# A one-core encoder trunk: DRAM copies of weight sums moved to ScalarE's queue, a fixed load order, and a fused closing step

## The chip, the cores and the metric

The kernel runs on one core of a Trainium2 chip. TensorE (PE) multiplies matrices into PSUM, VectorE (DVE) and ScalarE (ACT) do element-wise work, GpSimd (POOL) does a little of it and issues the accumulating DMAs, and SyncE (SP) does nothing but issue DMAs. ACT can issue DMAs too. Each engine runs its own instructions in the order that the program's scheduler has given them, and waits at semaphores for the others. The metric is the device time of one launch in microseconds, as the median of several runs.

## The reference: four layers over 256 tokens

The input is 256 tokens of 1024 channels in float32. Four layers follow each other. Each adds a token mixer and then a feed-forward block, both behind an RMS norm; a last RMS norm with a gain closes the trunk. Layers 0 and 3 mix by retention (four heads, per-head norm with `ret_gn_w` and `ret_gn_b`, a silu gate), layer 1 by a Conformer convolution of width 31, layer 2 by stick-breaking attention with 16 heads. The feed-forward block, which the change mostly touches, is

```
h = relu(rms_norm(x, norm_ffn[i]) @ ffn_w1[i])      # 256 x 4096
x = x + (h * h) @ ffn_w2[i]                         # 256 x 1024
```

All weights are float32, 220 MB in all, and every one of them passes from DRAM through the core in one launch.

## The kernel before

**Weights.** The host lays the weights out in the order of use, in 220 chunks of 128x2048 floats (1 MB), each of two units of 128x1024. `unit_hi` (lines 347 to 390) loads a chunk on SP's queue when its first unit is due (line 362) into one of three `raw` buffers, makes the high part of a unit on ACT (`wh`, line 388, rounding to the format that PE multiplies), and `unit_lo` makes the rest on DVE (`wl`, line 395). There are five `wh` and five `wl` buffers. A float32 product is three products of parts: high by high, high by low, low by high. Activations are split the same way.

**Down projection.** `down` (from line 775) computes `(h*h) @ ffn_w2`. Some of its 16 blocks of 256 rows are done plainly (lists `MIXED` and `REST`), the others (`FAST`) by a Strassen scheme: 7 products of 128x128 by 128x512 blocks instead of 8, three matmuls each (line 780). For that a unit needs, beside its blocks b21, b11, b22, b12, the sums t1 = b11+b12, t3 = b12+b22, t2 = t1+b22, t4 = t2+b21. `make_sums` (lines 399 to 411) has the DMA engines form m of the first three in a DRAM tile `sums`, long before they are needed: line 405 copies b12 into one or two places (256 or 512 KB, on SP's queue, kept in program order), line 406 adds b11 and b22 to it by an accumulating DMA on POOL's queue, and for m = 3 lines 408 and 409, also POOL's, make t2. `AHEAD` lists at which chunk's load each such job is issued: one list for each layer, one entry for each `FAST` block. There are 31 jobs: 7 with m = 2 in layer 0, 6 with m = 1 in layer 1, 9 with m = 3 each in layers 2 and 3. When the `FAST` unit itself is loaded, 768 KB come from the weights (line 362), t1 from `sums` (line 365), and t3 and t2 into two of ten buffers called `t` (line 368). t4 is added on DVE (line 459), and lines 431 and 432 split the sums.

**Closing.** After the last `FAST` block the sums that were gathered in PSUM are combined (lines 823 to 830). C[0,1] and C[1,1] are completed there; C[0,0] and C[1,0], the left half of the columns for the two halves of the tokens, still take the plain blocks of `REST`. Then line 857 adds `e1` to C[0,0] and line 858 subtracts `u` from C[1,0] on DVE, in place in PSUM, and `scaled` (line 872) multiplies both by the row scale `r2` on ACT into `t` buffers. PE meanwhile does the first `REST` block of the right half, and then transposes the scaled tiles (line 885), which line 892 adds to the residual. The last layer (`final`) has its own hook, which squares and scales instead of transposing.

**Order of the work.** A scheduler orders the instructions of each engine by a timing model; within stages marked as manual the order is the program's. In stick-breaking attention PE and ACT are manual and DVE is not. `keep_in_program_order` keeps an instruction behind the one that the program traced just before it on the same engine, and says nothing of later ones, which may still be drawn ahead; `issue_after` puts a block's instructions behind a given one of the same engine. In the retention layers line 1147 loads the gain and the bias of a head's norm (`gn`) on SP's queue, in program order.

Of the kernel before, what the change touches and what calls it, by code (L numbers as in the profile page):

```python
# [12 lines left out]
ALU = mybir.AluOpType  # L13
# [48 lines left out]
AHEAD = {  # L62
    0: [(n, 2) for n in (26, 27, 28, 38, 40, 42, 45)],
    1: [(n, 1) for n in (81, 83, 85, 87, 89, 91)],
    2: [(n, 3) for n in (110, 112, 114, 116, 118, 121, 129, 133, 137)],
    3: [(n, 3) for n in (167, 170, 173, 176, 179, 182, 192, 196, 199)],
}
OUT_ORDER = [(kb, p) for g in (0, 2) for kb in range(4) for p in (g, g + 1)]
# [185 lines left out]
class Trunk:  # L254
# [92 lines left out]
    def unit_hi(self, key):  # L347
        nc = self.nc
        assert PLAN[self.un] == key, (PLAN[self.un], key)
        o = self.un % UPC  # L350
        if o == 0:
            n = self.un // UPC
            if n < len(self.first):
                self.rawt = self.first[n]
            else:
                self.rawt = self.raw.tile([P, RAWW], F32, name=self.nm("raw"), tag="raw")
                h = 1024 if n < 4 else UPC * 1024
                made = self.made.get((key[1], key[3])) if key[2] == "f" else None
                if made:
                    h = 1536  # L360
                for a in range(0, UPC * 1024 // h * h, h):
                    nc.sync.dma_start(self.rawt[:, a : a + h], self.w_d[n][:, a : a + h])
                if made:
                    d, m = made
                    nc.sync.dma_start(self.rawt[:, h : h + 512], d[:, :512])
                    self.fetched = [self.tmp() for _ in range(m - 1)]
                    for a, t in enumerate(self.fetched):
                        nc.sync.dma_start(t, d[:, 512 * (a + 1) : 512 * (a + 2)])
            for _ in range(min(2, len(self.later))):
                self.later.pop(0)()  # L370
            if self.un // UPC in JOBS:
                self.make_sums(*JOBS[self.un // UPC])
            if self.un // UPC in DECAY:
                i = DECAY.index(self.un // UPC) % RH
                if i == 0:
                    self.decay = self.cp.tile([P, RH * 384], F32, name=self.nm("decay"), tag="decay")
                n = i * 384
                self.tc.keep_in_program_order(
                    nc.sync.dma_start(self.decay[:, n : n + 384], self.cst_d[:, CCOL["D"] + n : CCOL["D"] + n + 384])
                )  # L380
        o = self.un % UPC
        src = self.rawt[:, o * 1024 : (o + 1) * 1024]
        hi = self.wp.tile([P, 1024], F32R, name=self.nm("wh"), tag="wh")
        lo = self.wp.tile([P, 1024], F32R, name=self.nm("wl"), tag="wl")
        n = 512 if self.un < 2 * UPC else 1024
        cuts = [slice(i, i + n) for i in range(0, 1024, n)]
        for s in cuts:
            nc.scalar.copy(hi[:, s], src[:, s])  # L388
        self.un += 1
        return hi, lo, src, cuts  # L390
# [8 lines left out]
    def make_sums(self, l, kb, m):  # L399
        nc = self.nc  # L400
        w = self.w_d[CHUNK[l, kb]]
        d = self.dram.tile([P, m * 512], F32, name=self.nm("sums"), tag=f"sums{l}_{kb}", bufs=1)
        n = min(m, 2)
        src = w[:, 1536:2048].unsqueeze(1).to_broadcast([P, n, 512])
        self.tc.keep_in_program_order(nc.sync.dma_start(v3(d[:, : n * 512], n, 512), src))
        nc.gpsimd.dma_start(d[:, : n * 512], w[:, 512 : 512 + n * 512], accum_op=ALU.add)  # L406
        if m == 3:
            nc.gpsimd.dma_start(d[:, 1024:], d[:, :512])
            nc.gpsimd.dma_start(d[:, 1024:], w[:, 1024:1536], accum_op=ALU.add)
        self.made[l, kb] = d, m  # L410
# [364 lines left out]
    def down(self, i, h, fast, begin, hook):  # L775
        nc = self.nc

        def triple(o, a, w, start=False, stop=False):
            for n, (l, r) in enumerate(((a[0], w[0]), (a[0], w[1]), (a[1], w[0]))):
                mm = nc.tensor.matmul(o, l, r, start=start and n == 0, stop=stop and n == 2, skip_group_check=True)  # L780
                self.tc.keep_in_program_order(mm)
            self.end = mm.ins

        def block(k, t):
            return tuple(h[k][:, o + t * P : o + (t + 1) * P] for o in (0, S))

        def plain(kb, c):
            w = self.unit(("ffn_w2", i, "a", kb, c * 512))
            return [tuple(v3(x, 2, 512)[:, kk] for x in w) for kk in range(2)]

        C = {}
        quick, mixed, late_kb = FAST[i], MIXED[i], REST[i]
        self.ahead = {}
        for _ in range(2):
            self.sum_ahead(i)
        for kb in mixed:
            if kb not in quick:
                for c in range(2):
                    w = plain(kb, c)
                    if kb == mixed[0]:  # L800
                        for t in range(2):
                            C[t, c] = self.acc()
                            if begin:
                                begin(c, t, C[t, c])
                    for kk in range(2):
                        for t in range(2):
                            triple(C[t, c], block(2 * kb + kk, t), w[kk], kb == mixed[0] and kk == 0 and not begin)
                continue
            w = self.fast_unit("ffn_w2", i, kb)
            s3, s2, s4 = fast[kb]  # L810
            a, z = kb == quick[0], kb == quick[-1]
            if a:
                p1, p5, p7, p6 = own = [self.mis() for _ in range(4)]
            k = 2 * kb
            for o, x, y in (
                (p1, block(k, 0), w[0]), (C[0, 0], block(k + 1, 0), w[1]), (C[0, 1], s4, w[2]), (p5, block(k, 1), w[3]),
                (p7, s3, w[4]), (p6, s2, w[5]), (C[1, 0], block(k + 1, 1), w[6]),
            ):
                extra = o in own
                triple(o, x, y, a and extra, z and extra)  # L820

        e1, e5, v, u, vq, uq = (self.bigt() for _ in range(6))
        nc.scalar.copy(e1, p1)
        nc.scalar.copy(e5, p5)
        nc.vector.tensor_sub(v, p6, e1)
        nc.vector.tensor_sub(u, v, p7)
        nc.vector.tensor_add(vq, v, e5)
        nc.vector.tensor_add(uq, u, e5)
        nc.vector.tensor_add(C[0, 1], C[0, 1], vq)
        closed = nc.vector.tensor_add(C[1, 1], C[1, 1], uq).ins  # L830

        hook(C, "gain")
        if i == 0:
            self.strip_t = []

            def fetch():
                d = self.strips[len(self.strip_t)]
                o = self.bigt()
                self.tc.keep_in_program_order(nc.sync.dma_start(o, d))
                self.strip_t.append(o)  # L840

            self.later = [fetch] * len(self.strips)

        for c in range(2):
            w, late = {}, late_kb[-2] if c else late_kb[-1] + 1
            steps = [(kb, kk, t) for kb in late_kb if kb < late for kk in range(2) for t in range(2)]
            steps += [(kb, kk, t) for t in range(2) for kb in late_kb if kb >= late for kk in range(2)]
            for kb, kk, t in steps:
                if kb not in w:
                    with self.tc.issue_after(closed) if c else nullcontext():  # L850
                        w[kb] = plain(kb, c)
                if c:
                    hook(C, (kb, kk, t))
                triple(C[t, c], block(2 * kb + kk, t), w[kb][kk], stop=(kb, kk) == (late_kb[-1], 1))
            if c == 0:
                with self.tc.issue_after(closed):
                    nc.vector.tensor_add(C[0, 0], C[0, 0], e1)
                    nc.vector.tensor_sub(C[1, 0], C[1, 0], u)
                hook(C, 0)
        return C  # L860


    def middle(self, i, h, fast, sums, nxt):
# [28 lines left out]
            nc.vector.tensor_add(x, x, a)  # L892

        def hook(C, at):
            if at == 0:
                for t in range(2):
                    scaled(C, t, 0)
                self.norm_begin()
            if at == (REST[i][1], 0, 0):
                for t in range(2):  # L900
# [26 lines left out]
    def final(self, i, h, fast):  # L927
# [12 lines left out]
                ))  # L940

        def hook(C, at):
            if at == "gain":
                for c in range(2):
                    gain.append(self.bigt())
                    nc.sync.dma_start(gain[c], self.fin_d[:, c * 512 : (c + 1) * 512])
            if at:
                return
            for t in range(2):
                q, g, sm = self.tmp(), self.tmp(), f[:, t : t + 1]  # L950
                nc.scalar.activation(out=q, in_=C[t, 0], func=AF.Square, accum_out=sm)
# [906 lines left out]
```

## Time and profile before

| | us |
|---|---|
| median of 3 runs | 1330.94 |
| the runs | 1328.36, 1330.94, 1335.21 |
| time of the profiled execution | 1330.45 |
| its span, first to last instruction | 1328.7 |
| PE busy / DVE busy / ACT busy / POOL busy | 1311.1 / 1088.6 / 882.6 / 212.5 |

The profile is of one execution. A row of the timeline gives the start in us from the span's start, the duration in us, the engine, the line of the kernel, the operation, out<-in, the shapes, how many instructions are merged, and in brackets the idle time of the engine before it and what ended it. "SPq" is a DMA issue on SP; its duration is that of the issue, not of the transfer. A row of waits gives who waited for whom, the total in us, how often, and the longest. In the chain of waits a row is start, duration, what. In a list of DMA issues the last number is the median time from issue to landing, in us.

### The profile page before, as it was taken

The numbers are of one execution on the slowest core, as the hardware profiler recorded it, in microseconds if no ns is written. First come the engines' busy times: TensorE is split into PE (matmuls) and PEld (weight loads), VectorE is DVE, ScalarE is ACT, GpSimd is POOL, SyncE is SP. The second block draws the span as 40 slices with busy tenths as digits, with TensorE's granted clock in tenths as the row PEclk, the third lists the DMA queues.
The fourth block names the chain that finished last, engine by engine and source line by source line (L and its number), as shares of the span: only waits on it lengthen the run. The fifth ranks groups of instructions, "written<-read, shape, count | busy, mean of one in ns | idle before, by whom it ended". The sixth has DMA issues, their size and how long they took to land.

```text
span 1328.7 us, 20675 instructions
## 1 busy us (share of the span) xinstructions
PE 1311.1 (99%) x7661; PEld 1127.1 (85%) x7661; DVE 1088.6 (82%) x1903; ACT 882.6 (66%) x1451; POOL 212.5 (16%) x240
## 2 busy tenths in 40 slices
PE   9999999999999999999999999999999999999998
PEld 7988888888889898888778898888888888888876
DVE  7988777888888588789878588888898767899977
ACT  7555546886666477866758678867765554667764
POOL 3554421000009120010011011000121110100000
PEclk9999999999999999999999999999999999999999
DMA  8566786966675658688698658777568987687673
GB/s 310 206 217 231 244 281 194 298 210 227 233 300 145 206 192 242 220 247 260 208 256 214 210 185 281 245 257 268 214 207 247 267 247 237 196 256 249 226 278 111
DMA packets 76038, 309.58 MB, mean 233 GB/s; under 512 B 8480, under 2 KB 13728, under 8 KB 52512
## 3 DMA queue, kind: packets, MB, share of 16 engines
q1 hardware_dynamic: 63552, 274.43, 59.4%
q0 software_dynamic: 11520, 31.20, 12.3%
q10 hardware_dynamic: 864, 2.62, 0.6%
q8 instruction: 60, 0.98, 0.3%
q14 instruction: 42, 0.34, 0.1%
HBM read 301.57 MB, written 45.45 MB: 261 GB/s over the span
## 4 chain that ended last, share of the span: by engine, by line
PE 95%; DMA 2%; DVE 1%; ACT 1%; issue 1%; SPq 0%; ACTq 0%; DVEq 0%
PE acc L643 22%; PE acc L780 17%; PE acc L639 11%; PE mis L780 7%; PE acc L1207 5%; PE acc L1209 5%; PE acc L1208 5%; PE acc L623 3%; PE acc L624 3%; PE acc L625 3%; PE mis L643 2%; DMA raw<-in_w 1%; PE acc L1375 1%; PE mis L639 1%; PE acc L1508 1%; DMA big<-in_gn 1%
## 5 line engine op out<-in xcount | busy, mean ns | idle before, releaser
L395 DVE TENSOR_TENSOR wl<-raw,wh 128x1024 fp32r<-128x1024 f32 (+1 forms) x406 | 495.4, 1232 | 105.0 <-ACT wh L388 103.5
L388 ACT CAST wh<-raw 128x1024 fp32r<-128x1024 f32 (+1 forms) x406 | 418.4, 1041 | 201.0 <-PE acc L1209 61.7
L643 PE MATMUL acc<-z,wh 128*128 128x512 f32 x1152 | 399.4, 393 | 0.0
L639 PE MATMUL acc<-z,wl 128*128 128x256 f32 x1152 | 317.9, 281 | 0.0
L643 PEld LDWEIGHTS acc<-z,wh 128*128 128x128 f32 x1152 | 214.2, 187 | 47.1
L639 PEld LDWEIGHTS acc<-z,wl 128*128 128x128 f32 x1152 | 216.9, 189 | 2.4 <-DVE t L668 0.3
L780 PE MATMUL acc<-wh,big 128*128 128x512 f32 x632 | 208.6, 391 | 0.0
L780 PEld LDWEIGHTS acc<-wh,big 128*128 128x128 f32 x632 | 118.6, 188 | 24.4
L1207 PE MATMUL acc<-wh,z 128*128 128x512 f32 x352 | 139.1, 396 | 0.0
L1209 PE MATMUL acc<-wh,z 128*128 128x512 f32 x352 | 137.8, 391 | 0.0
L1208 PE MATMUL acc<-wl,z 128*128 128x512 f32 x352 | 137.7, 391 | 0.0
L780 PE MATMUL acc<-wl,big 128*128 128x512 f32 x316 | 123.0, 389 | 0.0
L667 ACT COPY t<-acc 128x256 f32<-128x256 f32 x154 | 53.0, 371 | 51.6 <-PE acc L643 50.0
L431 ACT CAST wh<-t 128x512 fp32r<-128x512 f32 x102 | 60.3, 619 | 39.2 <-PE acc L780 12.0
L1207 PEld LDWEIGHTS acc<-wh,z 128*128 128x128 f32 x352 | 66.6, 189 | 15.4 <-issue 2.2
L1209 PEld LDWEIGHTS acc<-wh,z 128*128 128x128 f32 x352 | 66.4, 189 | 14.9 <-issue 0.8
L1208 PEld LDWEIGHTS acc<-wl,z 128*128 128x128 f32 x352 | 66.6, 189 | 13.4
L432 DVE TENSOR_TENSOR wl<-t,wh 128x512 fp32r<-128x512 f32 x102 | 65.9, 684 | 5.9 <-ACT wh L431 5.9
L780 PEld LDWEIGHTS acc<-wl,big 128*128 128x128 f32 x316 | 59.4, 188 | 12.1
L668 DVE TENSOR_TENSOR t<-acc,t 128x256 f32<-128x256 f32 x154 | 59.1, 415 | 12.4 <-ACT t L667 12.3
L406 POOL DMA_DIRECT2D sums<-in_w x31 | 25.9, 870 | 256.6 <-DMA sums<-in_w 256.6
L623 PE MATMUL acc<-z,wh 128*128 128x256 f32 x224 | 63.7, 284 | 0.0
(307 smaller groups left out, 2352.8 us busy)
## 6 DMA issues: line engine op xcount, KB each, us to landing
raw<-in_w SPq DMA_DIRECT2D x183, 1024.0 KB, 5.3
raw<-in_w SPq DMA_DIRECT2D x31, 768.0 KB, 4.5
sums<-in_w SPq DMA_DIRECT2D x25, 512.0 KB, 8.2
sums<-in_w POOLq DMA_DIRECT2D x25, 512.0 KB, 8.1
t<-sums SPq DMA_DIRECT2D x43, 256.0 KB, 5.4
raw<-sums SPq DMA_DIRECT2D x31, 256.0 KB, 4.9
sums<-in_w POOLq DMA_DIRECT2D x24, 256.0 KB, 7.3
strip<-st POOLq DMA_DIRECT2D x36, 128.0 KB, 4.0
```

Source lines behind the costliest of these rows:

```text
L388: nc.scalar.copy(hi[:, s], src[:, s])
L395: self.lo_ins = self.nc.vector.tensor_sub(lo[:, s], src[:, s], hi[:, s]).ins
L431: nc.scalar.copy(h[:, c], t)
L432: self.lo_ins = nc.vector.tensor_sub(g[:, c], t, h[:, c]).ins
L623: nc.tensor.matmul(o, wh[:, kk, cs], ah, start=st, stop=False, **kw)
L639: mm = nc.tensor.matmul(ps[m][:, :S], wl[:, kk, cs], a[:, :S], start=first and kk == 0, stop=False, **kw)
L643: nc.tensor.matmul(ps[m], wh[:, kk, cs], a, start=False, stop=last and kk == 3, **kw)
L668: nc.vector.tensor_add(o[:, s], ps[m][:, :S], o[:, s])
L780: mm = nc.tensor.matmul(o, l, r, start=start and n == 0, stop=stop and n == 2, skip_group_check=True)
L1207: nc.tensor.matmul(ps[t], zh[:, s], wh[:, kk], start=k == 0, stop=False, skip_group_check=True)
L1208: nc.tensor.matmul(ps[t], zh[:, s], wl[:, kk], start=False, stop=False, skip_group_check=True)
L1209: nc.tensor.matmul(ps[t], zl[:, s], wh[:, kk], start=False, stop=k == 7, skip_group_check=True)
```

## The change

There are five edits.

1. The copy that begins a job of weight sums (line 405) is issued on ACT's queue instead of SP's; it stays in program order, now of ACT.
2. The loads of a `FAST` unit that has sums made ahead (lines 362, 365, 368) are kept in program order, except those of a layer's first two `FAST` blocks.
3. The closing of C[0,0] and C[1,0] and their scaling become one DVE operation each for the layers 0 to 2: `e1` and `u` are first scaled by `r2` on ACT (two new activations, issued right after the closing), and then C * r2 plus or minus the scaled block goes from PSUM into a `t` buffer.
4. In the last layer the two DVE operations of lines 857 and 858 stay, moved into its hook.
5. The jobs of layer 2 are issued at other chunks: at 112, 114, 116, 118, 120, 128, 131, 134, 137 instead of 110, 112, 114, 116, 118, 121, 129, 133, 137.

```diff
-    2: [(n, 3) for n in (110, 112, 114, 116, 118, 121, 129, 133, 137)],
+    2: [(n, 3) for n in (112, 114, 116, 118, 120, 128, 131, 134, 137)],
@@ unit_hi
-                for a in range(0, UPC * 1024 // h * h, h):
-                    nc.sync.dma_start(self.rawt[:, a : a + h], self.w_d[n][:, a : a + h])
+                parts = [
+                    (self.rawt[:, a : a + h], self.w_d[n][:, a : a + h]) for a in range(0, UPC * 1024 // h * h, h)
+                ]
                 if made:
                     d, m = made
-                    nc.sync.dma_start(self.rawt[:, h : h + 512], d[:, :512])
+                    parts.append((self.rawt[:, h : h + 512], d[:, :512]))
                     self.fetched = [self.tmp() for _ in range(m - 1)]
-                    for a, t in enumerate(self.fetched):
-                        nc.sync.dma_start(t, d[:, 512 * (a + 1) : 512 * (a + 2)])
+                    parts += [(t, d[:, 512 * (a + 1) : 512 * (a + 2)]) for a, t in enumerate(self.fetched)]
+                for o, d in parts:
+                    load = nc.sync.dma_start(o, d)
+                    if made and key[3] not in FAST[key[1]][:2]:
+                        self.tc.keep_in_program_order(load)
@@ make_sums
-        self.tc.keep_in_program_order(nc.sync.dma_start(v3(d[:, : n * 512], n, 512), src))
+        self.tc.keep_in_program_order(nc.scalar.dma_start(v3(d[:, : n * 512], n, 512), src))
@@ down
-        hook(C, "gain")
+        C["e1"], C["u"] = e1, u
+        hook(C, "open")
...
                 with self.tc.issue_after(closed):
-                    nc.vector.tensor_add(C[0, 0], C[0, 0], e1)
-                    nc.vector.tensor_sub(C[1, 0], C[1, 0], u)
-                hook(C, 0)
+                    hook(C, 0)
@@ middle, hook
+            if at == "open":
+                for t, a in enumerate((C["e1"], C["u"])):
+                    b = self.bigt()
+                    nc.scalar.activation(out=b, in_=a, func=AF.Copy, scale=r2[:, t : t + 1])
+                    y["open", t] = b
             if at == 0:
-                for t in range(2):
-                    scaled(C, t, 0)
+                for t, op in enumerate((ALU.add, ALU.subtract)):
+                    y[t, 0] = self.tmp()
+                    nc.vector.scalar_tensor_tensor(
+                        out=y[t, 0], in0=C[t, 0], scalar=r2[:, t : t + 1], in1=y["open", t], op0=ALU.mult, op1=op
+                    )
                 self.norm_begin()
@@ final, hook
-            if at == "gain":
+            if at == "open":
...
+            nc.vector.tensor_add(C[0, 0], C[0, 0], C["e1"])
+            nc.vector.tensor_sub(C[1, 0], C[1, 0], C["u"])
```

## The prediction, made before the changed kernel was built or run

> **What bounds the kernel now.** I read the page first, then the waits of PE, then the chain and the timelines around each wait.
>
> ```profile
> span 1328.7 us, 20675 instructions
> PE 1311.1 (99%) x7661; PEld 1127.1 (85%) x7661; DVE 1088.6 (82%) x1903; ACT 882.6 (66%) x1451; POOL 212.5 (16%) x240
> PE 95%; DMA 2%; DVE 1%; ACT 1%; issue 1%; SPq 0%; ACTq 0%; DVEq 0%
> ```
>
> PE is busy for 1311.1 of 1328.7 us, and the chain that ends last is PE for 95%. The change takes no matmul away and adds none. All that it can win is idle PE time, 1328.7 - 1311.1 = 17.6 us, and stretches in which PE ran slowly. So the second view is who PE waited for:
>
> ```profile
> PE mis L1690 <- DVE t L1680: 2.4, 2, 2.1
> PE mis L1393 <- issue: 2.1, 2, 1.2
> PE mis L885 <- ACT t L872: 1.9, 2, 1.2
> PE mis L311 <- POOL t L283: 1.3, 1, 1.3
> PE mis L780 <- DVE wl L432: 1.2, 1, 1.2
> PE mis L1163 <- DVE t L1160: 1.1, 1, 1.1
> ```
>
> Line 311 is the start and line 1393 the convolution; no edit touches either. The other four rows, 2.4 + 1.9 + 1.2 + 1.1 = 6.6 us, are what an edit may reach. I go through them by edit.
>
> **The copies on ACT's queue, and layer 2's jobs.** The longest wait, in stick-breaking attention, is told by these rows (chain, issues, timeline, one window):
>
> ```profile
> 662.34 0.58 SPq L405 DMA_DIRECT2D sums<-in_w  x1
> ```
> ```profile
> 664.24 11.63 DMA raw<-in_w
> ```
> ```profile
> sums<-in_w SPq DMA_DIRECT2D x1, 512.0 KB, 11.1
> ```
> ```profile
> raw<-in_w SPq DMA_DIRECT2D x183, 1024.0 KB, 5.3
> ```
> ```profile
> 667.77 1.04 ACT L388 CAST wh<-raw 128x1024 fp32r<-128x1024 f32 x1
> ```
> ```profile
> 675.96 1.05 ACT L388 CAST wh<-raw 128x1024 fp32r<-128x1024 f32 x1 [4.97 <-DMA raw<-in_w]
> ```
> ```profile
> 677.04 1.22 DVE L395 TENSOR_TENSOR wl<-raw,wh 128x1024 fp32r<-128x1024 f32 x1 [3.48 <-ACT wh L388]
> ```
> ```profile
> 680.18 0.33 PE L1690 MATMUL mis<-cst,t 128*128 128x128 f32 x1 [2.12 <-DVE t L1680]
> ```
> ```profile
> 681.44:684.85 3.41, 3.41 (x11) 2.74 (x10) 0.73 (x2) 3.37 (x7) 0.00 (x0) 0.50 0.57 165
> ```
>
> A sums copy is issued on SP at 662.34 and lands 11.1 us later, at 673.4. The weight load behind it on the same queue, issued at 664.24, takes 11.63 us where 5.3 is the median, and lands at 675.9, 2.4 us after the copy: it stood behind it. ACT then waits 4.97 us, DVE (whose `wl` stands in the middle of the q/k norm) 3.48 us, and PE 2.12 us and once more, 2.4 in all. The last row shows what follows: for 3.41 us after the wait the granted clock is 0.50, which costs 3.41 x (1 - 0.50) = 1.7 us of PE time. On ACT's queue the copy no longer stands ahead of that load. ACT is in program order there, and reaches the place only at the `wh` of that chunk's first unit, at 667.77, 5.4 us after 662.34; the job at chunk 110, whose last accumulation ran beside this load, is gone too. The load needs to land 2.4 us earlier, before 673.5; with the median's 5.3 us it lands at 669.5. So I take 2.4 + 1.7 = 4.1 us. Bounds: 0, if the load is as late as now, and 4.1.
>
> By the Trainium skill (TensorE: Matmul & The Clock Gate, Part 1) the clock falls to half after an idle window of about 3.4 us. PE's wait here was shorter, and the clock fell all the same; by the page's rule this wait would cost no clock, and the sum would be 1.7 us smaller. Page and row differ, and the row decides.
>
> The same queue order stands in layer 3's retention:
>
> ```profile
> 1083.88 10.71 DMA big<-in_gn
> ```
> ```profile
> 1083.27 0.57 SPq L405 DMA_DIRECT2D sums<-in_w  x1
> ```
> ```profile
> 1094.70 1.41 DVE L1156 SCALAR_TENSOR_TENSOR t<-mis,G,big 128x512 f32<-128x512 f32 x2 [5.58 <-DMA big<-in_gn]
> ```
> ```profile
> 1100.33 0.84 PE L1163 MATMUL mis<-cst,t 128*128 128x128 f32 x5 [1.13 <-DVE t L1160]
> ```
>
> The `gn` loads are issued 0.6 us behind a sums copy and take 10.71 us; DVE waits 5.58 us for them and PE 1.13. This copy belongs to a chunk that SP fetches three chunks ahead; on ACT it comes behind the `wh` of the chunk before it, after these loads. PE needs them 1.1 us earlier. I take 1.1; bounds 0 and 1.1.
>
> What the move adds is an issue on ACT, 31 times:
>
> ```profile
> L405 SPq DMA_DIRECT2D sums<-in_w x31: 501/569/1968, 142.1 to 1188.9; - x31
> ```
>
> 0.57 us each on SP, 31 x 0.57 = 17.6 us in all on ACT, which has 1328.7 - 882.6 = 446 us to spare. Behind each issue queue the next `wh` copies, for which DVE's `wl` and then PE wait; the cover is ACT's run-ahead, up to five `wh` buffers. Below nothing it can't go; if no cover were left it is 17.6 us. I take 0, since no long wait of PE names ACT's `wh` today. POOL's accumulations (line 406) wait for the copy, so they start later too; POOL's other work that PE needs soon is the q/k sums of retention:
>
> ```profile
> 997.41 0.81 POOL L406 DMA_DIRECT2D sums<-in_w  x1 [6.99 <-DMA sums<-in_w]
> ```
> ```profile
> 1000.94 0.75 POOL L1030 TENSOR_TENSOR big<-t 128x256 f32<-128x256 f32 x1 [1.97 <-ACT t L1021]
> ```
>
> POOL sat idle for 1.97 us ahead of the second, so a copy that is 5.4 us later could push that sum by 5.4 - 1.97 = 3.4 us; between 0 and 3.4 I take 0, as PE does other heads' work in between.
>
> **Closing and scaling in one operation.** The wait of 1.2 us at line 885 is layer 1's:
>
> ```profile
> 645.50 0.68 DVE L858 TENSOR_TENSOR acc<-acc,big 128x512 f32<-128x512 f32 x1
> ```
> ```profile
> 646.53 1.04 ACT L388 CAST wh<-raw 128x1024 fp32r<-128x1024 f32 x1 [0.21 <-PE acc L780]
> 647.48 0.68 ACT L872 ACTIVATE t<-acc,r 128x512 f32<-128x512 f32 x1
> ```
> ```profile
> 648.22 0.55 PE L885 MATMUL mis<-cst,t 128*128 128x128 f32 x3 [1.19 <-ACT t L872]
> ```
> ```profile
> 376.80 0.44 PE L885 MATMUL mis<-cst,t 128*128 128x128 f32 x2 [0.74 <-ACT t L872]
> ```
> ```profile
> L1156 DVE SCALAR_TENSOR_TENSOR t<-mis,G,big 128x512 f32<-128x512 f32 x16 | 11.3, 746 | 13.7 <-DMA big<-in_gn 13.6
> L857 DVE TENSOR_TENSOR acc<-acc,big 128x512 f32<-128x512 f32 x4 | 2.8, 689 | 0.0
> ```
>
> DVE had C[1,0] ready at 646.18, but ACT put a `wh` copy of 1.04 us ahead of the scaling, and PE waited 1.19 us. With the fused operation (0.746 us by its kind on PSUM, for 0.689) DVE delivers the scaled tile itself at about 646.3, before PE is done with the first tile's transposes. So 1.2 us go; bounds 0 and 1.2. DVE pays 2 x 0.06 us in each of three layers, ACT trades two scalings of 0.68 for two of the same shape that nothing waits for until the plain blocks are through. The other wait, 0.74 us at 376.80, is for the right half's scaling, which stays.
>
> **The fixed load order.** The wait at line 780 lies in layer 3:
>
> ```profile
> 1278.46 0.33 SPq L362 DMA_DIRECT2D raw<-in_w  x1
> ...
> 1283.95 0.33 SPq L362 DMA_DIRECT2D raw<-in_w  x1
> ...
> 1284.81 0.94 SPq L368 DMA_DIRECT2D t<-sums  x2
> ```
> ```profile
> 1292.49 0.69 DVE L459 TENSOR_TENSOR t<-t,raw 128x512 f32<-128x512 f32 x1 [3.86 <-DMA t<-sums]
> ```
> ```profile
> 1293.84 0.50 PE L780 MATMUL mis<-wl,sum 128*128 128x512 f32 x1 [1.21 <-DVE wl L432]
> ```
>
> DVE stood at line 459, the t4 of the last `FAST` unit, for 3.86 us until that unit's t loads of 1284.81 had landed, with `wl` of an earlier unit queued behind it; PE wanted those. Today the t loads of units run ahead of their own raw loads and fill the `t` buffers. In fixed order each comes behind its raw load, one raw load (1283.95 - 1278.46 = 5.5 us) later, so buffers are held for less time, but a t load that must wait for a buffer now holds back the raw load behind it. Whether DVE's order changes is the scheduler's; the scheduler will see the last t loads later and so has less reason to draw that t4 ahead. I take 1.2 as gone; bounds 1.2 gained and, if the wait comes up in each of the four layers, 3 x 1.2 = 3.6 lost.
>
> **The sum**, against the profiled execution's 1330.45 (span 1328.7 and 1.75 around it; 0.5 below the median of the runs shown): 4.1 + 1.1 + 1.2 + 1.2 = 7.6 us off. The scheduler orders everything anew, and the old order has one accidental wait that no edit explains, 0.74 at 376.80; I add one more of that size. 1330.45 - 7.6 + 0.7 = 1323.55, so 1323.5. A measurement of this kernel can tell about 0.5%, 6.65 us of 1330.94, from no change; the bound is 1324.3, and the forecast is just beyond it.
>
> **The rivals.** *Shared engines*: the copies leave SP's queue but not the DMA engines, so the weight load at 664.24 and the `gn` loads land as late as now. Then only the closing and the order gain: 1330.45 - 2.4 + 0.7 = 1328.8. For it: the accumulations on POOL's queue run beside the loads today. Against it: the load landed 2.4 us after the copy, less than half of the median's 5.3, so its bytes moved mostly after the copy's. It decides if the load lands after 673.5. The Trainium skill (DMA: Bandwidth & Descriptors, "Issuing engines are not separate DMA queues") speaks for this rival: DMAs from different engines run on the same 16 DMA engines and interleave, and another issuing engine saves only issue time.
>
> *New waits*: the new order and the held-back raw loads bring waits as at 1293.84 in all four layers, 4.8 us where one of 1.2 was: 1330.45 - 4.1 - 1.1 - 1.2 + 3.6 = 1327.65, so 1327.7. For it: SP would wait for `t` buffers in order. Against it: raw loads land in 5.3 us and are issued three chunks ahead.
>
> *ACT's issue time on the path*: the 31 issues delay `wh` copies that PE is waiting for: 1330.45 - 6.9 + 17.6 = 1341.2, slower by 0.8%. It needs at least (6.65 + 6.9) / 0.57 = 24 of the 31 to be uncovered, or issues nearer to the longest on SP, 1.97 us. For it: in attention ACT is in program order and can't draw other work ahead. Against it: ACT is busy for 66%.
>
> **How the numbers follow.** Forecast 0.51, shared engines 0.19, new waits 0.20, ACT's issues 0.10. The forecast's own range is 1320 to 1326.5: with all of 7.6 and the 0.74 gone as well it is 1322.1, and the lowest of the three runs stood 2.6 below the median; at the other end 3 us of further waits. About two thirds of it, 0.35, lie below 1324.3, and 0.06 of the two next cases, where they come singly and small. So faster by over 0.5%: 0.41. The rest of these three, 0.49, is within 0.5%, less 0.02 for several new waits with a clock drop: 0.47. Slower: 0.12. The range reaches from 1320 to 1331.5, over both middle rivals and 2.7 us of scatter, and leaves out ACT's issues and some of both ends.
>
> **What would show it.** Right: no PE wait at line 1690 over 0.5 us and no window of clock 0.50 between 640 and 700; the load behind chunk 112 landing within 8 us; no PE wait at 1163; line 885 waiting for DVE, or not at all, in layer 1; ACT's idle time smaller by about 17 us and PE's waits not naming `wh`. Wrong: the load of the attention stage still over 11 us (shared engines); new rows PE <- DVE wl or ACT wh of over 1 us in the down projections (new waits); PE waiting for ACT `wh` right behind an ACT issue.

## The result, and the profile after

The changed kernel takes 1335.76 us (median of 20 runs, 1332.79 to 1338.69), the kernel before 1328.35 us (20 runs, 1324.79 to 1335.21): ratio 1.0054, 95% interval 1.0044 to 1.0065. It is slower by about half a per cent; the forecast was 1323.5 and the range ended at 1331.5. The profiled execution after took 1336.21 us. These are lines of its page:

```profile
span 1334.4 us, 20667 instructions
PE 1311.9 (98%) x7661; PEld 1126.7 (84%) x7661; DVE 1089.1 (82%) x1903; ACT 883.1 (66%) x1451; POOL 213.4 (16%) x240
PE 88%; DMA 6%; DVE 3%; ACT 1%; issue 1%; SPq 1%; DVEq 0%; POOLq 0%; ACTq 0%
```

The busy times are those of before to within 1 us. The span grew by 5.7 us, and the chain that ends last is PE for 88% where it was 95%, and DMA for 6% where it was 2%. Who PE waited for, as total, times and longest:

```profile
PE mis L784 <- ACT wh L435: 5.9, 1, 5.9
PE mis L1406 <- issue: 2.8, 2, 2.1
PE mis L888 <- ACT t L875: 2.4, 2, 1.4
PE acc L784 <- DVE wl L436: 1.6, 2, 1.0
PE mis L784 <- DVE wl L399: 1.5, 3, 1.2
```

Lines moved: 784 was 780 (the matmuls of the down projections), 888 was 885, 1406 was 1393, 435 and 436 were 431 and 432, 399 was 395. Two of the waits that the prediction meant to remove are gone, those at 1690 (now 1703) and 1163 (now 1176). A wait of 5.9 us in a down projection is new, and `wl` stands in two rows there, with five waits of at most 1.2 us, where it stood in one with a single wait.

PE does the same 7661 matmuls in both kernels, and in the same order but for 153 places in the retention layers, so where time was lost can be read off directly: take the start of the n-th matmul in both traces and see how the difference grows. In us, after minus before: convolution +0.68, layer 1's down projection **+7.93**, the beginning of attention **-4.21**, layer 2's down projection **+3.92**, layer 3's retention -1.35, layer 3's down projection -0.56, all other stretches together -0.66; in sum +5.75.

**Layer 1's down projection.** Its six jobs make only t1 ahead of time (m = 1), for six of its eight `FAST` blocks. The t3 of each `FAST` block is made just in time by another helper: SP loads b12 into a `t` buffer (line 421, before 417) and POOL's queue adds b22 to it (line 422, before 418). Four such loads open the stage. These are POOL's rows around the start of the stage (570.0 before, 570.2 after), after and then before; the brackets give the idle time before the row and what ended it:

```profile
570.21 0.81 POOL L410 DMA_DIRECT2D sums<-in_w  x1 [19.68 <-DMA sums<-in_w]
577.89 0.81 POOL L410 DMA_DIRECT2D sums<-in_w  x1 [6.87 <-DMA sums<-in_w]
581.33 3.58 POOL L422 DMA_DIRECT2D t<-in_w  x4 [2.62 <-DMA t<-in_w]
```
```profile
547.04 0.81 POOL L406 DMA_DIRECT2D sums<-in_w  x1 [10.51 <-DMA sums<-in_w]
576.48 3.58 POOL L418 DMA_DIRECT2D t<-in_w  x4 [28.63 <-DMA t<-in_w]
```

Before, the last job's accumulation was issued at 547.04 and POOL's queue was empty when the stage began. After, two accumulations of jobs stand there, at 570.21 and 577.89, and the stage's own come at 581.33 instead of 576.48. The DMA issues from 570.2 to 572.5 (KB each, median us to landing), after:

```profile
t<-in_w SPq DMA_DIRECT2D x4, 256.0 KB, 10.3
sums<-in_w POOLq DMA_DIRECT2D x1, 256.0 KB, 10.3
sums<-in_w ACTq DMA_DIRECT2D x1, 256.0 KB, 7.1
```

and before, from 570.3 to 572.5:

```profile
t<-in_w SPq DMA_DIRECT2D x4, 256.0 KB, 5.8
```

The same four loads land after 10.3 us beside a job's copy and accumulation, and after 5.8 us without. What hangs on them, after (chain, ACT, PE):

```profile
581.33 7.99 DMA t<-in_w
```
```profile
589.34 1.14 ACT L435 CAST wh<-t 128x512 fp32r<-128x512 f32 x2 [12.11 <-DMA t<-in_w]
```
```profile
590.01 0.79 PE L784 MATMUL mis<-wh,big 128*128 128x512 f32 x1 [5.86 <-ACT wh L435]
```

The first sum lands at 581.33 + 7.99 = 589.3, ACT splits it, and PE has been idle for 5.86 us. Before, ACT made this `wh` at 581.31, in time. So the sum is issued 4.85 us later, since its load landed later, and is then under way for 7.99 us where it was 4.8. Why the two jobs came so late is told by their issues, after and before:

```profile
565.14 0.50 ACTq L409 DMA_DIRECT2D sums<-in_w  x1
...
569.73 0.72 ACT L671 COPY t<-acc 128x256 f32<-128x256 f32 x2 [0.37 <-PE acc L647]
570.26 0.52 ACTq L409 DMA_DIRECT2D sums<-in_w  x1
570.35 1.05 ACT L392 CAST wh<-raw 128x1024 fp32r<-128x1024 f32 x1
```
```profile
541.45 0.50 SPq L405 DMA_DIRECT2D sums<-in_w  x1
```

The last copy was issued by SP at 541.45, and is issued by ACT at 570.26. SP, which only issues DMAs, had run chunks ahead of PE; ACT, in program order at this instruction, comes to it behind a copy for which it had waited for PE (569.73). The last row shows that the issue itself takes nothing from ACT's work: the next cast starts 0.09 us after the issue began, and ACT was not idle before it. The clock makes it worse (granted clock is the third column from the end):

```profile
584.20:586.65 2.45, 0.00 (x0) 0.00 (x0) 0.00 (x0) 0.00 (x0) 0.70 (x1) 1.00 1.05 254
586.65:593.45 6.80, 3.44 (x7) 2.43 (x8) 3.29 (x5) 3.68 (x6) 0.86 (x1) 0.50 0.98 174
593.45:596.00 2.55, 2.55 (x12) 2.08 (x11) 2.55 (x4) 1.35 (x3) 0.00 (x0) 0.99 0.15 26
```

Of the stretch at half clock PE works 3.44 us, which costs 3.44 x 0.5 = 1.7 us. 5.86 + 1.7 = 7.6 of the 7.9 us.

### The profile page after: what moved, and what is told of

Same layout as the page of the kernel before. It is cut to its first block, busy times and chain, and to the rows that moved or that the text cites. A ratio compares the mean times of both kernels' runs of the same rounds, so it can differ in the third digit from the quotient of the medians.

```text
span 1334.4 us, 20667 instructions
## 1 busy us (share of the span) xinstructions
PE 1311.9 (98%) x7661; PEld 1126.7 (84%) x7661; DVE 1089.1 (82%) x1903; ACT 883.1 (66%) x1451; POOL 213.4 (16%) x240
## 4 chain that ended last, share of the span: by engine, by line
PE 88%; DMA 6%; DVE 3%; ACT 1%; issue 1%; SPq 1%; DVEq 0%; POOLq 0%; ACTq 0%
PE acc L647 22%; PE acc L643 11%; PE acc L784 11%; PE acc L1220 6%; PE acc L1222 6%; PE acc L1221 6%; PE mis L784 5%; DMA t<-sums 3%; PE acc L627 3%; PE acc L628 3%; PE acc L629 3%; PE mis L647 2%; DVE wl L399 1%; DMA t<-in_w 1%; PE acc L1388 1%; PE mis L643 1%
## 5 line engine op out<-in xcount | busy, mean ns | idle before, releaser
L784 PE MATMUL mis<-wh,big 128*128 128x512 f32 x168 | 64.1, 396 | 5.9 <-ACT wh L435 5.9
```

## The experiments

Theory: the queue's effect is when a job is issued. ACT issues it late, its accumulations run into the loads of the stage that needs them, and PE waits. Rivals: the queue itself (ACT's issue time, order within SP's queue), the fixed load order, the fused closing. The table has, for each kernel, the difference from before in us by stage (matmul by matmul, one profiled execution each) and the ratio of times with its interval (20 runs of the change, 4 to 12 of each other kernel). The convolution is listed because no edit touches it: it moves by -2 to +2 us all the same, and shows how much of a single profile is scatter. There it is PE's wait on "issue" (line 1393 before), from none to 2.9 us in total, and in e7, e10 and e12 a stretch of half clock behind it.

| kernel | conv. | layer 1 down | attention | layer 2 down | layer 3 ret. | ratio (95%) |
|---|---|---|---|---|---|---|
| the change | +0.7 | +7.9 | -4.2 | +3.9 | -1.4 | 1.0054 (1.0044 to 1.0065) |
| e1_only_queue | +0.2 | +9.1 | -3.0 | +0.4 | -1.9 | 1.0041 (1.0022 to 1.0060) |
| e2_queue_back | -2.1 | +0.1 | -4.2 | +2.2 | -0.8 | 0.9988 (0.9976 to 1.0001) |
| e3_free_loads | -0.3 | +8.2 | -4.2 | +3.2 | -1.3 | 1.0044 (1.0024 to 1.0063) |
| e4_layer1_early | -0.3 | 0.0 | -4.2 | +1.8 | -1.9 | 0.9995 (0.9981 to 1.0008) |
| e5_late_on_sp | -1.6 | +8.2 | +0.1 | 0.0 | -0.7 | 1.0049 (1.0031 to 1.0066) |
| e6_jobs_early | -1.9 | 0.0 | -4.2 | +1.3 | -1.9 | 0.9969 (0.9955 to 0.9982) |
| e7_only_closing | +2.3 | 0.0 | +0.2 | +0.4 | -1.4 | 0.9997 (0.9987 to 1.0008) |
| e8_early_dve | -1.3 | 0.0 | -4.2 | +2.3 | -1.9 | 1.0004 (0.9992 to 1.0015) |
| e9_only_jobs | +0.6 | 0.0 | -3.3 | +0.9 | -1.4 | 0.9977 (0.9965 to 0.9988) |
| e10_queue_and_jobs | +2.3 | 0.0 | -4.2 | 0.0 | -1.9 | 0.9971 (0.9957 to 0.9985) |
| e11_early_on_sp | -0.5 | 0.0 | -4.2 | +0.2 | +0.2 | 0.9987 (0.9970 to 1.0004) |
| e12_early_free | +2.2 | 0.0 | -4.2 | +0.3 | -1.9 | 0.9949 (0.9933 to 0.9964) |

**e1: the queue alone, on the kernel before.**

```diff
-        self.tc.keep_in_program_order(nc.sync.dma_start(v3(d[:, : n * 512], n, 512), src))
+        self.tc.keep_in_program_order(nc.scalar.dma_start(v3(d[:, : n * 512], n, 512), src))
```

> The kernel before with one edit, the sums copies issued on ACT's queue. Late-copies theory (on ACT a job's copy is issued 11 to 44 us later than on SP, and the last jobs of a layer run into its down projection): layer 1's down projection longer by 6 to 9 us than before, the attention stage shorter by 3 to 5 us, layer 3's retention shorter by about 1 us; in all 1 to 5 us slower than before. Fixed-order theory (the pinned loads make the new waits): layer 1's down projection as before within 1 us, so 4 to 6 us faster in all.

1333.5 us against 1327.88. One wait, and the 31 copies (issue in ns, least, median and most; first and last):

```profile
PE mis L780 <- ACT wh L431: 5.6, 1, 5.6
```
```profile
L405 ACTq DMA_DIRECT2D sums<-in_w x31: 497/559/657, 153.2 to 1218.0; - x31
```

The loss comes with this one edit, within the intervals, and it is layer 1's. It is 9.1 us there, more than the change's 7.9, with a shorter wait: the half clock, from 590.17 to 597.00, falls on PE at work again from 590.51 on, and costs 6.49 x 0.5 = 3.2 us. The jobs are those of before, so each copy's delay can be read: the first 153.2 - 142.1 = 11.1 us, the last 1218.0 - 1188.9 = 29.1 us; over all 31 from 7.5 to 42.5 us, median 26.9. Of this, 5 to 10 us from layer 1's down projection on are the kernel's own lateness; against PE's place in the work the copies are 5.0 to 35.5 us late, median 24.2. The issue takes 0.56 us on ACT, as on SP.

**e2: the change with the copies on SP.**

```diff
-        self.tc.keep_in_program_order(nc.scalar.dma_start(v3(d[:, : n * 512], n, 512), src))
+        self.tc.keep_in_program_order(nc.sync.dma_start(v3(d[:, : n * 512], n, 512), src))
```

> The changed kernel with the copies back on SP's queue. Late-copies theory: the wait of 5.9 us in layer 1 and the waits of 1.2 and 1.0 us in layer 2's down projection go, so 8 to 13 us faster than the changed kernel; the attention stage has its wait of 2 to 4 us again, since the job at chunk 112 stands ahead of a weight load again, unless it was the job at 110 that made it. About 1325 to 1329 us. Fixed-order theory: the waits stay and it is as slow as the changed kernel, or slower by the 4 us of the attention stage.

1325.49 us against 1327.88. Layer 1's loss is gone, and attention keeps the whole gain of 4.2 us on SP's queue. So the gain of attention does not need ACT's queue. Layer 2's loss was expected to go as well, and 2.2 us of it stay.

**e3: the change without the fixed load order.**

```diff
-                    load = nc.sync.dma_start(o, d)
-                    if made and key[3] not in FAST[key[1]][:2]:
-                        self.tc.keep_in_program_order(load)
+                    nc.sync.dma_start(o, d)
```

> The changed kernel with the loads of the Strassen units free to be reordered again. Late-copies theory: layer 1's wait of about 6 us stays, total within 3 us of the changed kernel. Fixed-order theory: that wait is under 1 us, and the kernel is 6 to 9 us faster than the changed one; layer 2's 3.9 us may go with it.

1334.27 us against 1327.88, and the wait in layer 1 stays (lines are two lower):

```profile
PE mis L782 <- ACT wh L433: 5.6, 1, 5.6
```

The fixed order is not its cause.

**e4: the change with layer 1's jobs five chunks earlier**, still on ACT.

```diff
-    1: [(n, 1) for n in (81, 83, 85, 87, 89, 91)],
+    1: [(n, 1) for n in (76, 78, 80, 82, 84, 86)],
```

> The changed kernel with layer 1's six jobs five chunks earlier (76, 78, 80, 82, 84, 86), so that on ACT's queue their copies come about when they came on SP's before. Late-copies theory: layer 1's wait of 5.9 us goes and the kernel is 6 to 9 us faster than the changed one, about 1327 to 1330 us; layer 2's 3.9 us stay. Fixed-order theory: no change from the changed kernel beyond 2 us.

1326.91 us against 1327.88. POOL's first row of the stage:

```profile
575.67 3.58 POOL L422 DMA_DIRECT2D t<-in_w  x4 [28.62 <-DMA t<-in_w]
```

It was idle for 28.62 us before, as in the kernel before, and no wait of PE for line 435 is left. Same queue, earlier place: the loss is gone. Layer 2's jobs are those of the change, and yet its loss is 1.8 us here for 3.9: about 2 us of that figure change with the schedule or the execution alone.

**e5: the kernel before, copies on SP, layer 1's jobs five chunks later.**

```diff
-    1: [(n, 1) for n in (81, 83, 85, 87, 89, 91)],
+    1: [(n, 1) for n in (86, 88, 90, 92, 94, 96)],
```

> The kernel before, copies on SP's queue as ever, with layer 1's jobs five chunks later (86, 88, 90, 92, 94, 96), about as late as they are on ACT's queue. Lateness theory (what costs is when the last copies and accumulations run, not which engine issues them): layer 1's down projection 4 to 9 us longer than before with a wait of PE for the wh of a sum, so 4 to 9 us slower. Queue theory (ACT's issue or its own ring is what costs): layer 1 within 1 us of before.

1334.62 us against 1327.79, the change's loss without ACT's queue. PE's wait and POOL's rows:

```profile
PE mis L780 <- ACT wh L431: 5.4, 1, 5.4
```
```profile
575.95 0.81 POOL L406 DMA_DIRECT2D sums<-in_w  x1 [12.60 <-DMA sums<-in_w]
576.69 3.68 POOL L418 DMA_DIRECT2D t<-in_w  x4
```

This splits the mechanism. Here the four loads are hardly slower (6.4 us to landing, for 5.8), and POOL issues its first sum at 576.69, as before (576.48). But one job's accumulation stands right ahead of it on POOL's queue, and the first sum lands 10.3 us after its issue where it took 4.8 us (DMA issues at 576.69 here, and at 576.48 before):

```profile
t<-in_w POOLq DMA_DIRECT2D x1, 256.0 KB, 10.3
```
```profile
t<-in_w POOLq DMA_DIRECT2D x1, 256.0 KB, 4.8
```

One late job beside the first sum is enough for 5.4 us. e4 and e5 together settle it: lateness costs, on either queue. Whether the first sum is slow because the job's accumulation is ahead of it on POOL's queue, or only because it runs beside it, no run separates.

**e6: layer 2's last jobs earlier as well**, on e4.

```diff
-    2: [(n, 3) for n in (112, 114, 116, 118, 120, 128, 131, 134, 137)],
+    2: [(n, 3) for n in (112, 114, 116, 118, 120, 123, 126, 129, 132)],
```

> The changed kernel with layer 1's jobs five chunks earlier and layer 2's last four at 123, 126, 129, 132 instead of 128, 131, 134, 137. Late-copies theory: beside layer 1's wait, the 3.9 us that layer 2's down projection has lost go too, since its last accumulations land before that stage: 2 to 4 us faster than with layer 1's jobs alone moved, about 1323 to 1325 us. If layer 2's loss comes of the fixed order or of the fused closing: as with layer 1's jobs alone, about 1327 us.

1324.43 us against 1327.79: faster than both kernels. Its waits in the down projections:

```profile
PE mis L784 <- DVE wl L399: 0.9, 2, 0.7
...
PE acc L784 <- DVE wl L436: 0.6, 1, 0.6
```

Layer 2's loss is 1.3 us where the change had 3.9 and e4, on which this kernel builds, 1.8. That it was lateness alone is not borne out. Where the gain over e4 lies is not shown either: the two profiled executions took nearly the same, 1323.20 and 1322.80 us.

**e7: the fused closing alone**, edits 3 and 4 on the kernel before; its diff is the part of the change's from `down` on.

> The kernel before with the fused closing alone. Given-back theory (behind the wait that it removes, PE meets the right half's scaling, which ACT does behind four other activations): layer 1's wait of 1.2 us at the first transposes goes, a wait of 1.0 to 1.5 us at the transposes of the right half comes, total within 1 us of before. Prediction's theory: 1.2 us faster. Both are near what can be measured in the total; the profile tells them apart.

1327.63 us against 1327.79: worth nothing. Its wait at the transposes, and, in the change, ACT's rows and PE's in layer 1:

```profile
PE mis L884 <- ACT t L871: 2.4, 2, 1.4
```
```profile
657.69 0.91 ACT L546 ACTIVATE z<-head 128x256 fp32r<-128x256 f32 x2 [1.89 <-DVE head L895]
...
660.35 0.67 ACT L875 ACTIVATE t<-acc,r 128x512 f32<-128x512 f32 x1
```
```profile
661.07 0.33 PE L888 MATMUL mis<-cst,t 128*128 128x128 f32 x1 [1.44 <-ACT t L875]
```

and ACT's two rows in the kernel before:

```profile
649.47 0.91 ACT L542 ACTIVATE z<-head 128x256 fp32r<-128x256 f32 x2 [1.30 <-DVE head L892]
...
652.12 0.67 ACT L872 ACTIVATE t<-acc,r 128x512 f32<-128x512 f32 x1
```

The wait at the first tile's transposes (1.19 us) is gone as predicted. But what follows on the other engines comes no sooner. PE runs 8.2 us later here in the change, by what was lost up to this place, and by just that these rows are later: 657.69 - 649.47 = 8.22 and 660.35 - 652.12 = 8.23. ACT waits there for DVE's residual add (line 895, before 892), which comes behind two `wl` of DVE in both kernels; then it makes the next norm's statistics (lines 546 and 557), and the right half's scaling stands behind them. PE gets to that scaling's transposes sooner and waits there: 1.44 us, and 0.96 in layer 0 where it was 0.74.

**e8: that scaling on DVE**, on e6.

```diff
-                scaled(C, 0, 1)
+                scaled(C, 0, 1, (slice(0, 512), "dve"))
```

> The changed kernel with the earlier jobs of layers 1 and 2, and the right half's first scaling (C[0,1]) on DVE instead of ACT in layers 0 to 2. Given-back theory: the waits of 0.96 us in layer 0 and 1.4 us in layer 1 at the right half's transposes go, 1.5 to 2.4 us faster than the same kernel with that scaling on ACT, if DVE is free there; if DVE's own queue (residual adds, wl) is as late as ACT's, no gain.

1328.87 us, ratio 1.0004 where e6 has 0.9969: slower, not faster, and the wait grew (DVE and PE in layer 1, and the clock behind the wait, third column from the end):

```profile
652.50 0.69 DVE L562 TENSOR_TENSOR t<-t,t 128x512 f32<-128x512 f32 x1
653.11 0.75 DVE L877 TENSOR_SCALAR t<-acc,r 128x512 f32<-128x512 f32 x1
```
```profile
653.91 0.93 PE L888 MATMUL mis<-cst,t 128*128 128x128 f32 x4 [2.24 <-DVE t L877]
```
```profile
654.15:657.56 3.41, 3.41 (x11) 2.80 (x10) 0.84 (x2) 0.12 (x1) 0.00 (x0) 0.50 0.00 0
```

DVE takes the scaling behind its own share of the same statistics, the last of which (line 562) ends later than ACT's. PE's waits at the transposes are 5.3 us in all where e6 has 2.4, and the half clock costs 3.41 x 0.5 = 1.7 us more: together 4.6 us, and the times differ by 4.4. Another engine does not help when the queue in front is the same work.

**e9: layer 2's job places alone**, edit 5 on the kernel before, copies on SP.

```diff
-    2: [(n, 3) for n in (110, 112, 114, 116, 118, 121, 129, 133, 137)],
+    2: [(n, 3) for n in (112, 114, 116, 118, 120, 128, 131, 134, 137)],
```

> The kernel before with the changed kernel's list of layer 2's jobs and nothing else (copies on SP). Theory (the job that began at chunk 110 made the attention wait, through its accumulations beside the weight load; the queue order did not): the wait of 2.1 us at line 1690 and the half clock behind it go, 4.1 us, about 1324, ratio 0.997. Rival (as the prediction has it, the load was late since it stood behind a copy on SP's queue): a copy still stands ahead of a load there, the wait stays and the ratio is 1.000 with the load landing after over 11 us.

1324.37 us against 1327.16. The wait in attention falls from 2.4 us to

```profile
PE mis L1690 <- DVE t L1680: 0.5, 2, 0.3
```

and a copy still stands between two weight loads on SP's queue: a load at 662.70, the copy at 663.08, the next load at 664.97. The copy's time to landing, and that of the load behind it (chain):

```profile
sums<-in_w SPq DMA_DIRECT2D x1, 512.0 KB, 7.6
```
```profile
664.97 9.74 DMA raw<-in_w
```

The load ahead of the copy took 4.8 us, here as before. Before, POOL also had a job's accumulation out at that time, which is gone here with the job of chunk 110:

```profile
662.20 0.81 POOL L409 DMA_DIRECT2D sums<-in_w  x1 [2.72 <-DMA sums<-sums]
```

Without that job the load is 11.63 - 9.74 = 1.9 us quicker, and PE's wait shrinks by the same 1.9 us. Most of the load's lateness stays, and neither theory has it whole. The same load in the other kernels, with PE's wait at that place, shows what each part does:

| what stood beside the load | its time, us | PE's wait, us |
|---|---|---|
| copy ahead on SP, job of 110 (before, e5, e7) | 11.6 to 11.9 | 2.4 to 2.6 |
| copy ahead on SP, job of 110 gone (e9, e11, e2) | 9.7, 8.5, 8.1 | 0.5, none, none |
| no copy ahead, the accumulation of 110 beside it (e1) | 10.0 | 0.8 |
| no copy ahead, job of 110 gone (the change, e3, e4, e6, e8, e10, e12) | 5.1 to 6.0 | none |

Either part alone brings the load near the time at which PE begins to wait; the two together cost 2.4 us and a stretch of half clock. This one line of job places is worth as much as the best of the first eight kernels, within the intervals.

**e10: copies on ACT and e6's job places, without the fixed order and the closing**: the diff of e1, with e4's and e6's lists, on the kernel before.

> The kernel before with the copies on ACT and with the earlier job places of e6_jobs_early in layers 1 and 2; neither the fixed load order nor the fused closing. Theory (only the issue times of the jobs matter; the other two edits are worth nothing net): as e6_jobs_early, ratio 0.9955 to 0.9985. Rival (fixed order and closing each bring their 1.2 us): 2.4 us slower than e6_jobs_early, ratio 0.9987 or more.

1324.55 us against 1327.16, ratio as e6's. The loss of layer 2's down projection is gone. The two left-out edits together bring nothing that the times show.

**e11: e6 with the copies on SP**, by e2's diff.

> e6_jobs_early with the copies back on SP's queue, which issues them about three chunks earlier still. Theory (a job must only be early enough; which queue issues it does not matter): within 1.5 us of e6_jobs_early, ratio 0.996 to 0.999, no wait over 2 us in the down projections. Rival (a copy ahead of loads on SP's queue holds them up, which ACT's queue avoids): new waits on weight or gn loads, such as 1.1 us at line 1176 and 2 us at line 1703, 3 to 4 us slower, ratio 1.000.

1325.16 us against 1327.16. No wait in the down projections, but one in retention that the eight kernels with copies on ACT do not have (nor has e9, with copies on SP):

```profile
PE mis L1176 <- DVE t L1173: 1.3, 1, 1.3
```

Its interval overlaps e6's and e10's, so whether ACT's queue has a merit of its own stays open; if it has one, it is of this size.

**e12: e6 without the fixed order**, by e3's diff, to see what was left of layer 2's loss.

> e6_jobs_early without the fixed order of the loads. It asks what is left of layer 2's loss once the jobs are early: e6_jobs_early is 1.3 us slower than the kernel before in layer 2's down projection, with PE waits of 0.7 and 0.6 us on wl, and e10_queue_and_jobs, which has neither the fixed order nor the fused closing, is not. Theory (the fixed order holds raw loads back there, the prediction's new waits): the loss of 1.3 us goes, ratio 0.996. Rival (it is not the fixed order, but the closing or just another schedule): the stage still loses 1 us or more, ratio 0.997 as e6_jobs_early.

1322.21 us against 1328.72, the best ratio of all, 0.9949. Layer 2's loss is 0.3 us and none of PE's waits names `wl`. This speaks for the fixed order holding back loads there; but the interval overlaps e6's and e10's, its profiled execution (1325.01 us) is slower than e6's, and with the late jobs (e3 against the change) leaving the order free brought only 0.7 us. From e10 it differs by the fused closing alone, which e7 found to be worth nothing; so the step from 0.9971 to 0.9949 has no cause that is shown. How layer 2's 3.9 us divide between job places, order and the accident of a new schedule stays open.

## Why the prediction was wrong, point by point

**The step that failed** is "What the move adds". It priced the issue on ACT (31 x 0.57 us, taken as 0) and gave the copy's lateness one row: 5.4 us, against POOL's work of line 1030. The 0 for the issue time was right: e4 has the same 31 issues and loses nothing, and in the change ACT's next operation follows without idle time in 26 of the 31 places. (ACT's busy time can't show it, for issues are not counted there.) The lateness was mis-sized, 26.9 us in the median where I read 5.4 from one place, and its price was looked for in one place only. For the copy from which it was read, 5.4 was right: in e1 that copy is 15.0 us later by the clock and 5.0 us against PE's place. It was not right for the others. I had noted that "POOL's accumulations (line 406) wait for the copy, so they start later too", and did not ask what else stands on POOL's queue when the last jobs of a layer come 29 us later: the sums of layer 1's own stage. That term, taken as 0 with 3.4 us as its upper end, measured 7.9 us: 5.86 of wait and 1.7 of half clock. One row of before had shown the margin: POOL idle for 28.63 us before 576.48, which the last copy's delay, 570.26 - 541.45 = 28.8 us, uses up. The other large term is layer 2's down projection, 3.9 us, which stood outside the sum, in the rival *New waits*; its cause is not settled. Of the signs named for being right, those of attention and of `gn`'s PE wait held; line 888 (885 before) still waits for ACT in layer 1, and PE's waits name `wh`.

**Attention** (4.1 us forecast): 4.2 came, and the reading was right in the main. Both of its reasons are real: the copy ahead holds the load up, and so does the accumulation of the job at 110. e1, which moves the copies alone, gained 3.0; e9, which changes layer 2's job places alone, so that none is at 110, 3.3; the change does both and gains 4.2. The gains do not add, since each alone takes most of PE's wait and all of the half clock.

By the Trainium skill (DMA: Bandwidth & Descriptors, "Issuing engines are not separate DMA queues") another issuing engine saves issue time only. In e1 the issue takes about as long as on SP (0.56 us, for 0.57); what changed is the time at which the transfers begin, by up to 42.5 us, and the loss in layer 1 came of that.

**Layer 3's `gn`** (1.1 us): PE's wait went, but not for my reason. The two loads at 1090.9 have no copy ahead of them on SP and are under way as long:

```profile
big<-in_gn SPq DMA_DIRECT2D x2, 256.0 KB, 10.8
```

It was 10.71 for the first of them before. In e7 and e9 a copy does stand ahead, and the first `gn` load takes 8.0 and 8.5 us. So the copy ahead does not by itself explain 10.7 us. DVE still waits for them, for a shorter time:

```profile
1101.35 1.41 DVE L1169 SCALAR_TENSOR_TENSOR t<-mis,G,big 128x512 f32<-128x512 f32 x2 [2.39 <-DMA big<-in_gn]
```

and the stage gains 1.4 us in e7 and e9 as well, which keep SP's queue. The cause of this gain is not settled.

**Closing** (1.2 us): the wait went and came back at the right half, since the scaling there waits for DVE's and ACT's own work, which the edit does not make sooner; e7 is 0.9997. That term took the right half's wait as fixed.

**Fixed order** (1.2 us in layer 3): that stage is 0.6 us better in the change, but e9 and e10, which have no fixed order, are 1.8 and 1.9 us better there. The gain is not the edit's.

**The rivals.** *New waits* named the place, the down projections, and the sign, rows of `wh` and `wl` over 1 us; but it laid them to the fixed order in all four layers at 4.8 us, and e3 shows that the large one is not the order's. *ACT's issue time* had the right direction and a time near the result (1341.2), by a mechanism that e1 and e4 refute: the same 31 issues stand in e4, and its ratio is 0.9995. *Shared engines* said that the load at 664.24 would land as late as now; it took 6.0 us, so by the sign given for it this rival failed. Its mechanism is partly borne out all the same: in e1 the load has no copy ahead and still takes 10.0 us beside an accumulation. The argument against it was read wrongly: a load that takes 5.3 us in the median and lands 2.4 us after the copy moved more than half of its bytes, by that measure, while the copy was still under way.

## What to carry to other kernels

When a DMA moves to a compute engine's queue, ask first when that engine reaches the instruction, not what the issue costs: a queue that only issues DMAs runs ahead by its buffers, a compute engine runs with its data. Work out the new issue time of the last of them, and look at every queue that takes up the transfer behind it, to see what it will then stand ahead of or beside. A gain that two edits both claim should be measured with each alone.

## What the runs showed of the hardware beside this

In layer 1 the clock fell to 0.50 at 586.65, about 2.5 us after PE went idle, while it was still waiting, and stayed there for 6.8 us, twice 3.41; in attention before, one stretch of 3.41 us followed a wait of 2.12 us. That fits a clock that is decided in fixed stretches of 3.41 us, by the one before. All fourteen traces bear it out. From the clock's first rise to its first fall it is 675.84 us before and 580.27 us in the change, 198 and 170 times 3.4133. Laid on this grid, up to the last matmul, a stretch at full clock in which PE was idle for 2.06 us or more was followed by half clock each time (11 places), and one in which it was idle for 1.88 us or less never was. So it matters where a wait falls. In the convolution PE waits once for 2.06 to 2.08 us in five of the kernels: in e7, e10 and e12 inside one stretch, and the clock halves; in the change and e9 across the border of two (0.56 + 1.51 and 1.47 + 0.61 us), and it does not. That is the difference between +2.2 to +2.3 and +0.6 to +0.7 us in the table.

The Trainium skill (TensorE: Matmul & The Clock Gate, Part 1) has such free-running windows, and the length agrees; that a whole window must be idle does not agree with these places, where from 2.06 us of idle time on were enough.
